# Stores on the ACT queue, loads on the SP queue, issued in pairs that GpSimd gates

## The chip, the cores and the metric

The kernel runs on one core of a Trainium2 chip. A core has compute engines that run independently of each other and meet through semaphores: VectorE (DVE in the profile), GpSimd (POOL), ScalarE (ACT) and TensorE (PE, not used here). SyncE (SP) does no arithmetic; it issues transfers. A transfer moves data between the chip's main memory (DRAM) and the core's on-chip memory, which has 128 partitions. An engine that issues a transfer puts it on its own queue, and the core's 16 DMA engines do the moving. A transfer has *landed* when all its parts have reported to a semaphore.

The metric is device time in microseconds, less being better.

## The reference

The input is a matrix of 8192 x 8192 numbers in float32. The reference is the gradient along a row:

```python
def reference(x):
    return np.gradient(x, axis=1)
```

For each row, an inner element of the result is `(x[j+1] - x[j-1]) / 2`. At the two borders it is the one-sided difference: `x[1] - x[0]` at the left and `x[m-1] - x[m-2]` at the right. 268.4 MB are read and as many written, and there is one subtraction and one halving for each element.

## The kernel before

Rows are cut into 32 sets of 256 rows. In a set each of the 128 partitions holds R = 2 neighbouring rows, so 16384 numbers or 64 KB. Three slots (NB = 3) hold the sets; set i lives in slot i % 3. A slot is 64 numbers longer than a set (SH = 64): the load puts its data at an offset of 64, and the result is written from offset 0 on in the same slot, so that each result is written behind the place still to be read.

A set goes through these steps, which all belong to slot i % 3:

1. The load (line 60, `load`), issued on SP's queue. It waits until the store of set i - 3, which used the same slot, has landed.
2. The border differences (line 70): GpSimd subtracts two numbers for each row, the left and the right border, into the small tile `ends`. This instruction is the one that waits for the load to land.
3. The inner differences (line 76): VectorE forms half the difference of the neighbours over the whole set in one instruction of 16382 elements for each partition. It waits for step 2.
4. The border copy (line 87): the two border numbers of each row are copied from `ends` into the result. VectorE does it in 20 sets, GpSimd in 12. It waits for step 3.
5. The store (line 89), issued on SP's queue. It waits for step 4.

The order is written out by hand (`tc.manual_schedule()`), and each engine takes its instructions in that order. The function `chain` tells the compiler's framework which earlier steps an instruction must wait for, so that no further waits are put in.

Loads and stores both stand on SP's one queue. The order on it is: loads 0, 1, 2; stores 0, 1, 2; loads 3, 4, 5; stores 3, 4, 5; and so on. The loads of the next three sets come after the third store of a group. An issue on SP whose wait isn't fulfilled holds up those behind it; transfers already issued go on.

Of the kernel before, what the change touches and what calls it, by code (L numbers as in the profile page):

```python
# [1 line left out]

# [4 lines left out]


@with_exitstack
def kernel(  # L10
    ctx: ExitStack,
    tc: tile.TileContext,
    x: bass.AP,
    out: bass.AP,
):

    nc = tc.nc
    P = nc.NUM_PARTITIONS
    n, m = x.shape
    R = 2
    NB = 3  # L30
    SH = 64
    W = R * m
    nsets = n // (P * R)
    f32 = x.dtype

    x_sets = x.rearrange("(s p t) m -> s p (t m)", p=P, t=R)
    out_sets = out.rearrange("(s p t) m -> s p (t m)", p=P, t=R)

    pool = ctx.enter_context(tc.tile_pool(name="pool", bufs=1))
    slots = [pool.tile([P, SH + W], f32, name=f"slot{k}", tag=f"slot{k}") for k in range(NB)]  # L40
    ends = pool.tile([P, nsets, R, 2], f32, name="ends", tag="ends")
    loads, stores = [], [None] * nsets
    in_front = {}

    def chain(i, ins, *needed):

        group, engine = f"slot{i % NB}", ins.ins.engine
        keep = [o.ins for o in needed]  # L50
        if in_front.get(engine, (None,))[0] == group:
            keep.append(in_front[engine][1])
        tc.declare_no_dep(ins.ins, group=group, keep=keep, reason="implied by the needed step")
        tc.add_to_no_dep_group(group, ins.ins)
        in_front[engine] = group, ins.ins
        return ins

    def load(i):
        b = slots[i % NB]
        ins = nc.sync.dma_start(out=b[:, SH : SH + W], in_=x_sets[i])  # L60
        loads.append(chain(i, ins, *([stores[i - NB]] if i >= NB else [])))

    with tc.manual_schedule():
        for i in range(NB):
            load(i)
        for i in range(nsets):
            b = slots[i % NB]
            xin = b[:, SH : SH + W].rearrange("p (t m) -> p t m", m=m)

            ins = nc.gpsimd.tensor_sub(  # L70
                out=ends[:, i, :, :],
                in0=xin[:, :, 1 : m : m - 2],
                in1=xin[:, :, 0 : m - 1 : m - 2],
            )
            at = [chain(i, ins, loads[i])]
            ins = nc.vector._custom_dve(  # L76
                dve_ops.TENSOR_TENSOR_REDUCE_SUB_MAX,
                out=b[:, 1 : W - 1],
                in0=b[:, SH + 2 : SH + W],
                in1=b[:, SH : SH + W - 2],  # L80
                s0=0.0,
                s1=0.5,
            )
            halved = chain(i, ins, *at)
            res = b[:, 0:W].rearrange("p (t m) -> p t m", m=m)
            placer = nc.gpsimd if i % 5 in (1, 3) and i < nsets - 2 else nc.vector
            ins = placer.tensor_copy(out=res[:, :, 0 : m : m - 1], in_=ends[:, i, :, :])  # L87
            placed = chain(i, ins, halved)
            ins = nc.sync.dma_start(out=out_sets[i], in_=b[:, 0:W])
            stores[i] = chain(i, ins, placed)  # L90
            if i % NB == NB - 1:
                for k in range(i + 1, min(i + 1 + NB, nsets)):
                    load(k)


# [1 line left out]
_INS = ['x']  # L97
_OUTS = [((8192, 8192), 'float32')]


# [23 lines left out]
```

## Time and profile before

| what | value |
|---|---|
| time, median of 3 runs | 1247.93 us (1247.32 to 1248.15) |
| span of the profiled execution, first to last instruction | 1245.7 us |
| moved | 268.44 MB read, 268.44 MB written |
| mean rate | 431 GB/s |
| VectorE busy | 554.6 us, 45% |
| GpSimd busy | 8.8 us, 1% |
| inner differences (line 76) | 32 x 17.224 us |
| issue to landing, median | load 58.0 us, store 40.4 us |

The profile is taken from one execution. The page gives that execution's span; no other time of it is given, and the median of the runs is 2.2 us above the span. "Idle" ahead of an instruction is time in which its engine had nothing to run, with the event that ended it. A queue's waits (SPq) are those of the sequencer that issues transfers. "Issue to landing" includes the time that a transfer stands behind others on its queue. In the timeline and the chain the first number is the start in microseconds from the beginning of the span, the second the duration. The DMA view counts packets: the pieces in which a DMA engine moves a transfer.

### The profile page before, as it was taken

What the parts mean: (1) busy time and instruction counts of PE and PEld (TensorE: products, weight loads), DVE (VectorE), ACT (ScalarE), POOL (GpSimd) and SP (SyncE); (2) the same over time, 40 slices, a digit from 0 to 9 for tenths busy, and PEclk for the clock granted to TensorE, in tenths of its full rate; (3) what the DMA queues carried; (4) which work ended last, traced back from release to release, by engine and by line L of the source; (5) the groups of instructions that cost most, each with busy time, mean ns of one, the idle gap of its engine ahead of it and who ended that gap; (6) DMA issues with size and microseconds to landing.
All of it is one profiled execution on the core that took longest, in us unless ns stands there. A gap on an engine that the chain in (4) does not pass through costs nothing.

```text
span 1245.7 us, 237 instructions
## 1 busy us (share of the span) xinstructions
DVE 554.6 (45%) x52; POOL 8.8 (1%) x48
## 2 busy tenths in 40 slices
DVE  2850583069009702850582079009603840591083
POOL 0000000000000000000000000000000000000000
DMA  9999999999999999999999999999999999999999
GB/s 404 438 436 423 427 431 438 438 438 436 436 427 431 425 438 436 425 434 436 429 434 436 434 436 434 436 434 438 419 436 436 434 438 438 431 434 429 429 410 404
DMA packets 9217, 536.88 MB, mean 431 GB/s; under 512 B 1024, under 2 KB 1024, under 8 KB 1024
## 3 DMA queue, kind: packets, MB, share of 16 engines
q1 hardware_dynamic: 9216, 536.88, 99.8%
q14 instruction: 1, 0.01, 0.0%
HBM read 268.44 MB, written 268.44 MB: 431 GB/s over the span
## 4 chain that ended last, share of the span: by engine, by line
another core or an unknown queue 74%; DVE 18%; DMA 3%; issue 2%; POOL 1%; SPq 0%; POOLq 0%
DVE slot L76 18%; DMA slot<-in_x_dram 3%; POOL ends L70 0%; POOL slot L87 0%; SPq L60 0%; POOLq L119 0%; DVE slot L87 0%
## 5 line engine op out<-in xcount | busy, mean ns | idle before, releaser
L76 DVE CUSTOM_DVE_ANT_0 slot<-slot 128x16382 f32<-128x16382 f32 x32 | 551.2, 17224 | 668.7 <-POOL ends L70 668.7
L70 POOL TENSOR_TENSOR ends<-slot 128x4 f32<-128x4 f32 x32 | 6.3, 198 | 989.6 <-DMA slot<-in_x_dram 989.6
L87 POOL COPY slot<-ends 128x4 f32<-128x4 f32 x12 | 2.3, 190 | 207.9 <-DVE slot L76 207.9
L87 DVE COPY slot<-ends 128x4 f32<-128x4 f32 x20 | 3.4, 172 | 0.7
L108 POOL MEMSET const-bfloat16-1.0<- 128x1 bf16 x1 | 0.1, 101 | 0.0
L108 POOL MEMSET const-uint8-127<- 128x1 uint8 x1 | 0.1, 101 | 0.0
L108 POOL MEMSET const-float32-0.0<- 128x1 f32 x1 | 0.1, 98 | 0.2 <-issue 0.2
L108 POOL MEMSET const-float32-1.0<- 128x1 f32 x1 | 0.1, 98 | 0.0
## 6 DMA issues: line engine op xcount, KB each, us to landing
slot<-in_x_dram SPq DMA_DIRECT2D x32, 58.0
out_dram<-slot SPq DMA_DIRECT2D x32, 40.4
```

Of the source, the lines that this page charges most:

```text
L70: ins = nc.gpsimd.tensor_sub(out=ends[:, i, :, :], in0=xin[:, :, 1 : m : m - 2], in1=xin[:, :, 0 : m - 1 : m - 2],)
L76: ins = nc.vector._custom_dve(dve_ops.TENSOR_TENSOR_REDUCE_SUB_MAX, out=b[:, 1 : W - 1], in0=b[:, SH + 2 : SH + W], in1=b[:, SH : SH + W - 2],
L87: ins = placer.tensor_copy(out=res[:, :, 0 : m : m - 1], in_=ends[:, i, :, :])
L108: nc = _bacc.Bacc("TRN2", target_bir_lowering=False, num_devices=1)
```

## The change

Three things change.

- Stores are issued on ScalarE's queue (`nc.scalar.dma_start`). Loads stay on SP's.
- Loads no longer go out in threes. Two are issued at the start; after that, the load of set i + 2 is issued beside the store of set i. The load itself has no wait on a store any more.
- GpSimd gates both. Before the border copy of set i (for i = 1 to 30) it does a small memset, `touch`, which waits until store i - 1 has landed. The border copy, which is now always GpSimd's, comes after it in GpSimd's order, and so does a second small memset for sets 0 to 29. The store waits for the border copy; the load waits for the second memset. The memsets write four numbers each in the free slot, in the region which the load then fills.

```diff
-    def load(i):
+    def load(i, *needed):
         b = slots[i % NB]
         ins = nc.sync.dma_start(out=b[:, SH : SH + W], in_=x_sets[i])
-        loads.append(chain(i, ins, *([stores[i - NB]] if i >= NB else [])))
+        loads.append(chain(i, ins, *needed))
+
+    def touch(i, at, *needed):
+        ins = nc.gpsimd.memset(slots[i % NB][:, at : at + 4], 0.0)
+        return chain(i, ins, *needed)
 
     with tc.manual_schedule():
-        for i in range(NB):
+        for i in range(NB - 1):
             load(i)
         for i in range(nsets):
...
             halved = chain(i, ins, *at)
             res = b[:, 0:W].rearrange("p (t m) -> p t m", m=m)
-            placer = nc.gpsimd if i % 5 in (1, 3) and i < nsets - 2 else nc.vector
-            ins = placer.tensor_copy(out=res[:, :, 0 : m : m - 1], in_=ends[:, i, :, :])
+            ahead = i + NB - 1
+            if 0 < i < nsets - 1:
+                touch(ahead, SH, stores[i - 1])
+            ins = nc.gpsimd.tensor_copy(out=res[:, :, 0 : m : m - 1], in_=ends[:, i, :, :])
             placed = chain(i, ins, halved)
-            ins = nc.sync.dma_start(out=out_sets[i], in_=b[:, 0:W])
+            ins = nc.scalar.dma_start(out=out_sets[i], in_=b[:, 0:W])
             stores[i] = chain(i, ins, placed)
-            if i % NB == NB - 1:
-                for k in range(i + 1, min(i + 1 + NB, nsets)):
-                    load(k)
+            if ahead < nsets:
+                load(ahead, touch(ahead, SH + 4))
```

## The prediction

> **What bounds the kernel now.** I read the page first, then the chain that ended last, then the waits, then single windows of the timeline and of the DMA view. The page settles the resource at once.
>
> ```profile
> span 1245.7 us, 237 instructions
> DVE 554.6 (45%) x52; POOL 8.8 (1%) x48
> DMA  9999999999999999999999999999999999999999
> DMA packets 9217, 536.88 MB, mean 431 GB/s; under 512 B 1024, under 2 KB 1024, under 8 KB 1024
> q1 hardware_dynamic: 9216, 536.88, 99.8%
> ```
>
> The reader should see that the 16 DMA engines never have a free slice, that everything runs on one queue (q1, SP's), and that VectorE is busy less than half the time. A transfer is 8.39 MB. There are 64 of them and 9216/64 = 144 packets in each: 9 for each engine, of which 8 are data (128 partitions of 64 KB over 16 engines) and one is the small packet at the end that reports the landing (64 x 16 = 1024 small ones). The timeline of the first set gives the pace.
>
> ```profile
> 0.74 1.33 SPq L60 DMA_DIRECT2D slot<-in_x_dram  x3
> 22.71 0.20 POOL L70 TENSOR_TENSOR ends<-slot 128x4 f32<-128x4 f32 x1 [22.27 <-DMA slot<-in_x_dram]
> 22.95 17.22 DVE L76 CUSTOM_DVE_ANT_0 slot<-slot 128x16382 f32<-128x16382 f32 x1 [22.95 <-POOL ends L70]
> 40.20 0.17 DVE L87 COPY slot<-ends 128x4 f32<-128x4 f32 x1
> 40.40 40.06 SPq L89 DMA_DIRECT2D out_dram<-slot  x3
> 42.04 0.20 POOL L70 TENSOR_TENSOR ends<-slot 128x4 f32<-128x4 f32 x1 [19.13 <-DMA slot<-in_x_dram]
> 59.56 0.19 POOL L87 COPY slot<-ends 128x4 f32<-128x4 f32 x1 [17.32 <-DVE slot L76]
> 62.44 0.20 POOL L70 TENSOR_TENSOR ends<-slot 128x4 f32<-128x4 f32 x1 [2.69 <-DMA slot<-in_x_dram]
> ```
>
> GpSimd's `ends` starts when a load has landed. Load 0 lands at 22.71, load 1 at 42.04, so a transfer that follows another on the queue takes 19.33 us, 2.416 us for a 64 KB packet of one engine. Load 2, behind which a store stands, takes 20.40. The chain shows the same place in a later set: 19.35 from the first load to the second, 20.05 to the third.
>
> ```profile
> 372.46 0.20 POOL ends L70
> 391.81 0.20 POOL ends L70
> 411.86 0.21 POOL ends L70
> ```
>
> Over the ten sets of three the third load's excess over the second is 1.07, 0.09, 0.18, 0.70, 0.52, 0.44, 0.11, 0.50, -0.01 and 0.01: 3.61 us in all. So the account of the span is: first landing 22.71, 63 more transfers at 19.33 (1217.8), together 1240.5; the last store lands at 1244.9, so 4.4 us are lost on the way, 3.6 of them at the change from loads to stores; then 0.8 of ending. The median of the three runs lies 1247.93 - 1245.7 = 2.2 us above the profiled span; the page gives no other time of that execution, and I add these 2.2 to every span below.
>
> The waits of SP's queue say why nothing is lost between transfers.
>
> ```profile
> SPq L89 <- DVE slot L87: 525.6, 20, 55.9
> SPq L60 <- DMA out_dram<-slot: 373.1, 29, 19.3
> SPq L89 <- POOL slot L87: 300.1, 12, 36.9
> ```
>
> SP waits almost always, but for one store or load while at least one other transfer lies on the queue, so its waits reach no DMA engine.
>
> **What the change can win.** Only the 4.4 us: no byte goes away. All of it would be 0.35%; a difference under 0.2% (2.5 us) can't be told from none by these runs.
>
> **What goes and comes at no cost.** The 20 border copies of VectorE (172 ns) become GpSimd's (190 ns): 18 ns each, behind transfers. The 60 memsets (touches) are new on GpSimd, at 0.10 us by the four constants' rows; 30 of them only follow the copy. Load 2 is no longer issued at 1.6 but at about 40.4, together with store 0. The ACT queue issues nothing now, so a store's issue there has no row; SP's rows are 332 to 424 ns, and it no longer stands in line with the loads. Behind the new waiting memset on GpSimd stand the border copy, the second touch and the next `ends`. The next load lands at about the time a pair is issued, `ends` and VectorE need 0.2 + 17.2 us, and the memset waits to the end of a pair of 2 x 19.33 = 38.7 us: VectorE is done some 20 us before the gate opens. If that cover went (a pair under 18 us), VectorE would be late next; it can't go, as a pair moves 16.8 MB.
>
> **What the gate adds.** Store k and load k+2 are issued when store k-1 has landed, 30 times (i = 1 to 30). In the old kernel something always lay behind the running transfer. Here only the rest of load k+1 does. Everything hangs on how much of it is left when store k-1 reports.
>
> How an engine serves two queues is shown by one event: the only packet of another queue in the span.
>
> ```profile
> DMA packets 16, 0.99 MB, mean 496 GB/s; under 512 B 0, under 2 KB 0, under 8 KB 0
> q1 hardware_dynamic: 15, 0.98, 114.2%
> q14 instruction: 1, 0.01, 1.0%
> ```
>
> This is the DMA view of the window 997 to 999. In the packet records the 8 KB instruction packet begins at 997.70, when one engine's 64 KB packet ends, and takes 0.31 us (1.0% of 32 engine-microseconds); the next 64 KB packet of that engine, in the middle of store 24, follows it and takes 2.69 instead of 2.42. So an engine turns to another queue after each 64 KB packet, and moves one packet at a time. A pair then goes store, load, store, load. If both begin on an idle engine, eight of each alternate, and the store's small reporting packet must wait for its turn behind the load's eighth packet. Both land together and the queues are empty. Do they begin so? Load 1 leaves its engines at about 41.0 to 41.6 (landing at 42.04, less the 0.4 us between the end of the last packet and the wait that sees it, as at the last store in the packet records). Store 0 is issued at 40.40, and the first load needed 1.0 us from its issue to its first packet: 41.4. So most engines are idle or about to be, and the alternation starts with no lead.
>
> The price of a gap, from rows: the first load was issued on an idle queue at 0.74 and landed at 22.71, 21.97 us, of which 19.33 are full pace: 2.64 for issue, first packet and landing. The smallest such value is the last store's, 20.9 less 19.33 = 1.6, part of it behind store 30. Between landing and issue lie GpSimd's memset 0.10, the border copy 0.19, and the hand-over 0.03, with a hand-over ahead of them of the same kind: 0.35. A gap is 1.95 to 3.0; I take 2.5, the middle, because the store comes first and its pace has no idle-queue row of its own. 30 x 2.5 = 75 (58 to 90). The 3.6 at the change to stores go, as in-queue changes end. 1245.7 + 75 - 3.6 = 1317, with 2.2: 1319. At the end nothing new: store 30 runs while VectorE does set 31, as now (load 31's `ends` at 1206.28, store 31's issue at 1224.0).
>
> **The price with no row: changing from load to store inside a pair.** Each engine does it 8 times in 31 pairs, 248 times. Ends: -0.01 to 1.07 us each by the ten sets, so 0 to 265; the packet after the instruction packet cost 0.27, which would be 67. A gain below nothing I exclude: packets of both kinds keep 2.42 us alike, so an engine's pace is the same either way. I take 0 for the point: in the last two sets, when engines had drifted apart, the change cost 0.0. The 0.27 row is nearer in kind, but it is one event, so it is a rival at full weight rather than part of the sum.
>
> **A page against the row.** The Trainium skill, "DMA: Bandwidth & Descriptors", section "Queues, rings and completion order", says an engine goes round its queues but drains a whole packet, typically 9 to 17 descriptors, before it switches. If that meant the nine descriptors of a transfer here, store and load would follow one another whole, the store would land 19 us ahead, no gap would open, and the sum would be 1244 to 1255; the one event in store 24 speaks against it, and I go by the event. The same page, "Issuing engines are not separate DMA queues", says that issuing from several engines saves only issue time: by it nothing is to be won.
>
> **The rivals.**
> - Gap and change both cost: 1319 + 67 = 1386. For it: the 2.69 us packet. Against: it is one packet, and the change was free in the last sets.
> - Not slower: the store's report goes with its eighth data packet, with no turn of its own. Then the store lands one packet, 2.42 us, ahead of the load. The way from its last packet to the next first packet is 0.4 + 0.35 + 1.0 = 1.75 us, less than 2.42, so no engine runs dry, as long as engines stand less than 0.67 apart. 1247.9 - 3.6 = 1244.3. It decides at that 0.67: load 1's ends were 0.6 apart.
> - The same with the change costing 0.27: 1244.3 + 67 = 1311.
> - The change doesn't do what it says: an engine finishes a queue's whole share before it turns, so the pair is no pair but store, load, as on one queue. 1244.3, and with 31 changes at the mean 0.36 it is 1255.
>
> **How the numbers follow.** Gap alone 40 in 100 (own range 1302 to 1334); gap and change 20; lead holds and change costs 8; lead holds free 13 (8 faster, 4 same, 1 slower); whole shares 12 (3 faster, 4 same, 5 slower); anything else, such as changes at 0.1 or over 0.4 us, 7, slower. Faster 11, same 8, slower 81. Range 1244 to 1390: below it lie about 5 (the free lead with the rest of the 4.4 us), above it about 12 (the dear half of the second case).
>
> **What would show it.** In the changed profile: gaps between pairs as a mean rate of about 408 GB/s (536.88 MB in 1317 us) instead of 431, first `ends` of consecutive sets about 41.2 us apart, a store's issue to landing of about 40 us and a load's about the same. If stores land about 2.4 us before loads and the period is 38.7, the lead holds. If stores land after about 21 us, shares drain whole. If the period is above 43, the change from load to store costs. I am wrong if the report needs no turn of its own, or if a mix of reads and writes moves faster than 19.33 us for 8.39 MB.

## The result, and the profile after

The changed kernel takes 1636.5 us (1634.0 to 1642.7 in five runs), against 1247.9 before. The ratio is 1.312, with a 95% interval of 1.310 to 1.314. The direction was forecast; the size was not: 1319 was predicted, with a range of 1244 to 1390. The profiled execution has a span of 1640.9 us, 395 more than before.

The page of the changed kernel, its size, its DMA queues and the issues:

```profile
span 1640.9 us, 323 instructions
DMA packets 9217, 536.88 MB, mean 327 GB/s; under 512 B 1024, under 2 KB 1024, under 8 KB 1024
q1 hardware_dynamic: 4608, 268.44, 47.2%
q10 hardware_dynamic: 4608, 268.44, 40.4%
slot<-in_x_dram SPq DMA_DIRECT2D x32, 51.5
out_dram<-slot ACTq DMA_DIRECT2D x32, 51.7
```

The bytes and packets are those of before, in equal parts on SP's queue (q1, loads) and ACT's (q10, stores). The shares give two losses. They add up to 87.6% of the 16 engines' span where it was 99.8%, so an engine is idle for 12% of the span on the mean, some 200 us. And the packets are slower. A share times 16 engines times the span, over 4096 data packets, is the mean time of a 64 KB packet: 0.472 x 16 x 1640.9 / 4096 = 3.03 us for a load's, 0.404 in its place 2.59 us for a store's, where it was 2.42. A load and the store beside it take the same time to land, 51.5 and 51.7 us.

One pair in the timeline:

```profile
92.65 0.10 POOL L53 MEMSET slot<- 128x4 f32 x1 [50.54 <-DMA out_dram<-slot]
92.69 0.19 POOL L82 COPY slot<-ends 128x4 f32<-128x4 f32 x1
92.81 0.10 POOL L53 MEMSET slot<- 128x4 f32 x1
92.91 52.59 ACTq L84 DMA_DIRECT2D out_dram<-slot  x2
92.94 52.55 SPq L49 DMA_DIRECT2D slot<-in_x_dram  x2
144.88 0.10 POOL L53 MEMSET slot<- 128x4 f32 x1 [51.80 <-DMA out_dram<-slot]
```

GpSimd's gate waits 50.5 us and then 51.8, and the store and the load are issued 0.03 us apart. From gate to gate it is 52.2 us, where two transfers at full pace need 38.7. The packet records (start, duration, queue and size of every packet) of pairs 0 to 29 split a pair, on the mean over pairs:

| step of a pair | us |
|---|---|
| 16 packets at full pace | 38.7 |
| packets slower than that (8 x 3.06 + 8 x 2.60) | 6.6 |
| start of the first packets, and what lies between packets | 1.3 |
| wait of the mean engine for the slowest (46.6 to 50.2) | 3.6 |
| from the last landing report to the next pair's first packet | 1.8 |
| sum | 52.0 |

The excess is 13.3 us a pair, about 400 us for 30; less the 3.6 us of old changes from load to store, that is the measured 395. The records don't name the engine of a packet, but they can be chained, as one packet begins where another ends. So read, the packets of an engine alternate, load, store, load, store, and its two landing reports come within about 0.01 us of each other. In the 29 pairs from pair 1 to 29 the first packet on all 16 engines is the load's, though the store was issued 0.03 us earlier; the store's eighth packet is the last, with the load's report and then the store's right behind it.

VectorE's work stays hidden, as the waits of the changed kernel say. GpSimd's border difference waited for a load only at the two loads of the start:

```profile
POOL slot L53 <- DMA out_dram<-slot: 1545.5, 30, 52.6
POOL ends L63 <- DMA slot<-in_x_dram: 23.7, 2, 22.2
```

### The profile page after: what moved, and what is told of

The parts are those of the page before. It is cut to its first block, busy times and chain, and to the rows that moved or that the text cites. A ratio compares the mean times of both kernels' runs of the same rounds, so it can differ in the third digit from the quotient of the medians.

```text
span 1640.9 us, 323 instructions
## 1 busy us (share of the span) xinstructions
DVE 551.1 (34%) x32; POOL 13.5 (1%) x128
## 4 chain that ended last, share of the span: by engine, by line
another core or an unknown queue 94%; DMA 2%; issue 1%; POOL 1%; SPq 0%; POOLq 0%
DMA slot<-in_x_dram 2%; POOL ends L63 0%; POOL slot L53 0%; POOL slot L82 0%; SPq L49 0%; POOLq L113 0%
## 5 line engine op out<-in xcount | busy, mean ns | idle before, releaser
L53 POOL MEMSET slot<- 128x4 f32 x60 | 6.1, 101 | 1545.5 <-DMA out_dram<-slot 1545.5
L82 POOL COPY slot<-ends 128x4 f32<-128x4 f32 x32 | 6.1, 190 | 34.6 <-DVE slot L69 34.6
## 6 DMA issues: line engine op xcount, KB each, us to landing
slot<-in_x_dram SPq DMA_DIRECT2D x32, 51.5
out_dram<-slot ACTq DMA_DIRECT2D x32, 51.7
```

The costliest lines, as they stand in the source:

```text
L53: ins = nc.gpsimd.memset(slots[i % NB][:, at : at + 4], 0.0)
L82: ins = nc.gpsimd.tensor_copy(out=res[:, :, 0 : m : m - 1], in_=ends[:, i, :, :])
```

## Experiments

### First theory: alternating on two queues is slow, and the gate adds a gap

Four kernels, each with one part of the change taken back or alone. The first puts the stores on SP's queue and keeps the gate.

```diff
-            ins = nc.scalar.dma_start(out=out_sets[i], in_=b[:, 0:W])
+            ins = nc.sync.dma_start(out=out_sets[i], in_=b[:, 0:W])
```

> The changed kernel with the gate, the memsets and the pairs as they are, but the stores back on SP's queue, each store ahead of the load beside it. On one queue the two can't alternate. Theory A (most of the loss of 389 us comes from the two queues being served in turn, and the gate costs because both transfers then end together): the store lands after about 20 us of a pair, the next pair is issued while the load still moves, nothing runs dry, and the time falls to 1244 to 1256 us (the lower end is 1247.9 less the 3.6 us of the old changes from load to store, the upper adds 31 changes at 0.36 us). Rival B (the gate through GpSimd costs by itself, whatever the queues): above 1300 us.

Measured: 1250.3 us (1248.9 to 1251.9), ratio 1.0021 (1.0012 to 1.0030). The gate, the memsets and the pairs cost 2.4 us by themselves; rival B falls. The store lands after 38.4 us, not 20, since the load of the pair before still lies ahead of it, but the queue never runs empty.

The second is the same on one queue with the load ahead of the store, so that the last transfer on the queue opens the gate.

```diff
-            ins = nc.scalar.dma_start(out=out_sets[i], in_=b[:, 0:W])
-            stores[i] = chain(i, ins, placed)
             if ahead < nsets:
                 load(ahead, touch(ahead, SH + 4))
+            ins = nc.sync.dma_start(out=out_sets[i], in_=b[:, 0:W])
+            stores[i] = chain(i, ins, placed)
```

> As the changed kernel, but both transfers on SP's queue with the load ahead of the store, so that the store that opens the gate is the last on the queue: a gap at each of 30 pairs and no alternation. Theory A: only the round trip from landing to first packet is left, 1.95 to 3.0 us at each of 30 gates by the prediction's rows, so 1247.9 + 58 to 90 = 1306 to 1338 us. Rival B (the dry gap itself is what costs 13 us a pair): about 1636 us.

Measured: 1369.0 us, ratio 1.097 (1.096 to 1.099): 121 us, 4.0 at each of 30 gates, above the forecast 1.95 to 3.0. The packet records give the rest: besides some 2.2 us in which an engine is idle, the first load packet of a pair takes 0.7 us more than 2.42 and the load's last packet, ahead of the store, 1.2 more. So this is what running empty costs on one queue, and it is far from 13.

The third leaves two queues and takes the gate away.

```diff
-            if 0 < i < nsets - 1:
-                touch(ahead, SH, stores[i - 1])
...
-                load(ahead, touch(ahead, SH + 4))
+                load(ahead, *([stores[i - 1]] if i else []))
```

> Two queues as in the changed kernel, no gate: a store goes out when its border copy is done, a load when the store that frees its slot has landed. The packets of both queues still alternate on each engine, but an engine that is done early has further work behind. Theory A: the alternation alone stays, by the packet durations of the changed kernel's records (about 2.60 us for a store's packet and 3.06 for a load's, against 2.42): 31 pairs of 8 x 5.66 = 45.3 us, about 1245 + 31 x 6.6 = 1450 us, and the wait for the slowest engine goes. Rival B (the gate is the cause): back near 1250 us. Rival C (the alternation is all of it, and the gate costs nothing more): near 1636 us.

Measured: 1253.1 us, ratio 1.0050 (1.0028 to 1.0072). Theory A falls here, and rival C with it. The page's queue lines of this run:

```profile
span 1256.1 us, 263 instructions
q1 hardware_dynamic: 4608, 268.44, 49.5%
q10 hardware_dynamic: 4608, 268.44, 49.3%
```

0.495 x 16 x 1256.1 / 4096 is 2.43 us a packet, and the records show load, store, load, store on each engine, at 2.418 us in the median of either kind. Alternating packet by packet costs next to nothing: the whole kernel is 5 us above the one before.

The fourth has no computation and no waits between the kinds: loads into two slots in turn, stores of a third slot of zeros. These lines stand in place of the old loop.

```diff
...
+        nc.gpsimd.memset(slots[2][:, 0:W], 0.0)
+        for i in range(nsets):
+            nc.sync.dma_start(out=slots[i % 2][:, 0:W], in_=x_sets[i])
+            nc.scalar.dma_start(out=out_sets[i], in_=slots[2][:, 0:W])
...
```

> No computation: 32 loads on SP's queue into two slots in turn and 32 stores of a third slot, which holds zeros, on ACT's queue, all as large as before. The result isn't the gradient. No transfer waits on one of the other kind, and each queue always holds another transfer. Theory A: the two queues alternate packet by packet and it takes about 1245 + 31 x 6.6 = 1450 us, loads' packets about 3.06 us and stores' 2.60. Rival B (gates and waits on landings are the cause, and two busy queues move at full pace): 1240 to 1250 us.

Measured: 1261.0 us, the median of ten runs: three at 1245, one at 1255.5 and six from 1260 to 1265. The packets are again near 2.42. In the profiled run, one of the long ones, 14 engines end within 1.6 us of each other and the other two some 19 and 20 us later. The spread of a store's 16 reports grows from 1.4 to 22 us over that run, and the end waits for the last engine. The median is above rival B's 1240 to 1250, but theory A's 1450 is far off: two queues alternate freely.

### Second theory: it takes both queues running empty

If alternating is free and the gate is free, it must be the two together: both queues end at once at each gate and are filled again together. First, VectorE was taken out.

```diff
-            ins = nc.vector._custom_dve(
...
-            halved = chain(i, ins, *at)
-            res = b[:, 0:W].rearrange("p (t m) -> p t m", m=m)
+            halved = at[0]
+            res = b[:, SH : SH + W].rearrange("p (t m) -> p t m", m=m)
...
-            ins = nc.scalar.dma_start(out=out_sets[i], in_=b[:, 0:W])
+            ins = nc.scalar.dma_start(out=out_sets[i], in_=b[:, SH : SH + W])
```

> The changed kernel without VectorE's work: gate, two queues and pairs stay, the border copy writes into the loaded data and the store sends that. The result isn't the gradient. Theory D (the loss comes of the two queues both running empty at each gate and being filled again together; VectorE has no part in it): about 1636 us, between 1600 and 1660. Rival V (VectorE's reads and writes of on-chip memory slow the packets): clearly shorter, near 1400 us or below, and packets near 2.42 us.

Measured: 1588.9 us, in two runs. VectorE has no part in the slow pace (rival V falls). The time is below the 1600 to 1660 of theory D, and the run shows why, and how the kernel gets there. Without VectorE's 17 us the first store starts early, with the loads still far from done. Windows of about one pair each; the last two columns are the DMA share and GB/s:

```profile
30.00:70.00 40.00, 0.46 (x4) 1.00 1.02 441
70.00:114.00 44.00, 0.47 (x4) 1.00 0.99 429
114.00:158.00 44.00, 0.46 (x4) 1.00 0.99 429
158.00:206.00 48.00, 0.56 (x5) 1.00 0.86 350
206.00:258.00 52.00, 0.07 (x1) 1.00 0.87 323
258.00:311.00 53.00, 0.84 (x8) 1.00 0.86 317
```

For three pairs all is at full pace, and then it falls to the changed kernel's. By the packet records an engine's load reports 27, 19, 9, 2 and then 0 us after the store of its pair: between one store's report and the next store's first packet the engine serves loads alone, and the load catches up at each gate. Once it has caught up, both queues are empty at the gate, and it stays so. The changed kernel starts without that lead.

Next, free streams, without gates or computation, that start together on empty queues (a dry start) and never run empty again. These lines too stand in place of the old loop.

```diff
...
+        nc.sync.dma_start(out=slots[2][:, 0:W], in_=x_sets[0])
+        nc.gpsimd.tensor_copy(out=slots[0][:, 0:4], in_=slots[2][:, 0:4])
+        for i in range(nsets):
+            nc.scalar.dma_start(out=out_sets[i], in_=slots[2][:, 0:W])
+            if i + 2 < nsets:
+                nc.sync.dma_start(out=slots[i % 2][:, 0:W], in_=x_sets[i + 2])
...
```

> No gates and no computation: one load, and when it has landed a stream of 30 loads on SP's queue and a stream of 32 stores on ACT's start together on empty queues, as a pair of the changed kernel does, and go on without ever running empty. The result isn't the gradient. Theory D: the packets are slow (about 3.1 and 2.6 us) only after the common start, for some tens of us, and then settle at 2.42: the total is 1245 to 1275 us. Rival Y (a load and a store that start together and go in step stay slow for good, as they always touch the same piece of their sets): 30 pairs of 45 to 50 us, 1400 to 1500 us.

Measured: 1227.7 us for 63 transfers, one less than the expected 1245 to 1275 allowed for. On each engine the first two packets take 3.1 to 4.2 us, the others 2.42. Rival Y falls. This run was read as a sign for theory D; a later run shows how narrow it was.

Then the gate itself, with sets of half the size (R = 1, six slots), so that a pair can be issued while the one before still moves.

```diff
-    R = 2
-    NB = 3
+    R = 1
+    NB = 6
...
-        for i in range(NB - 1):
+        for i in range(NB - 2):
...
-            ahead = i + NB - 1
-            if 0 < i < nsets - 1:
-                touch(ahead, SH, stores[i - 1])
+            ahead = i + NB - 2
+            if 2 <= i < nsets - 1:
+                touch(ahead, SH, stores[i - 2])
```

> Sets of half the size (32 KB packets, 64 sets, six slots); two queues, pairs and GpSimd's gate as in the changed kernel, but the gate of pair i waits for store i-2, not i-1, so a whole pair is still moving when the next is issued. The small sets alone cost GpSimd and VectorE nothing that shows. Theory D (running empty is the cause): 1245 to 1265 us. Rival Q (issuing store and load together on two queues is the cause, empty or not): over 1400 us.

> As the run with the gate two back, but the gate waits for store i-1 as in the changed kernel: both queues run empty at each of 62 gates. Theory D: each gate costs again what it cost with large sets, 389/30 = 13 us, if the cost belongs to the empty start (62 x 13 = 800, about 2050 us), or half of it in the slow packets, if these are slow by the byte: 62 x (13 - 6.6/2) = 600, about 1850 us. Rival Q: the same time as the run with the gate two back.

The second of the two has the same sizes and the gate on store i - 1, with NB - 1 in both places of the diff. Measured: 1247.3 us with the gate two back (ratio 0.9997, 0.9987 to 1.0007) and 1445.8 us with the gate one back. Queue lines of the page, first two back, then one back:

```profile
q1 hardware_dynamic: 9216, 268.44, 50.0%
q10 hardware_dynamic: 9216, 268.44, 49.9%
```

```profile
q1 hardware_dynamic: 9216, 268.44, 47.5%
q10 hardware_dynamic: 9216, 268.44, 43.1%
```

So the emptying is needed for the loss: one gate's depth is worth 198 us, and rival Q falls. But the price was wrong. It is 3.2 us on the mean of 62 gates, neither 13 nor 10; the first six still had loads left, and over the 56 that found every engine idle it is 3.5. With 32 KB packets only a load's first packet after such a gate is slow (2.4 us instead of 1.21), the others keep pace, and the engines end a pair within 0.7 us of each other. Something more makes the large pieces slow for a whole pair.

### What keeps the 64 KB packets slow

The streams that settled had their first store issued 0.25 us ahead of the load; the changed kernel has 0.03. Three kernels varied the start and the size of the pieces, which is the size of a data packet. The first: the free streams with the load ahead, by a GpSimd memset that the stores also wait for.

```diff
+        nc.gpsimd.memset(slots[2][:, 0:600], 0.0)
         for i in range(nsets):
-            nc.scalar.dma_start(out=out_sets[i], in_=slots[2][:, 0:W])
             if i + 2 < nsets:
                 nc.sync.dma_start(out=slots[i % 2][:, 0:W], in_=x_sets[i + 2])
+            nc.scalar.dma_start(out=out_sets[i], in_=slots[2][:, 0:W])
```

> As the run of free streams after a common dry start, but the load starts first: ACT's stores also wait for a small GpSimd memset of about 0.5 us. The result isn't the gradient. What is asked is why the packets in a pair of the changed kernel stay slow for all 46 us, when those of the free streams settled after two packets. Theory O (the order: in the changed kernel the load's packet moves first, in the free streams the store's did): the packets stay slow well beyond the first two, and the total is above 1260 us, up to 1450. Rival K (one transfer on each queue is too little stock for pieces of 64 KB, whatever the order): settles after two packets again, 1225 to 1235 us, as 63 transfers are moved.

Measured: 1231.3 us, two slow packets on each engine and then 2.42. That the load is first doesn't by itself make the packets slow. But the start differs from the changed kernel's in another way: with the load 0.67 us ahead, each engine moves two load packets before the first store packet.

The second: the changed kernel, the memset that releases the load 2400 numbers wide (`touch` gets the width as a parameter).

```diff
...
-                load(ahead, touch(ahead, SH + 4))
+                load(ahead, touch(ahead, SH + 4, n=2400))
```

> The changed kernel with the second memset, which lets the load go, made 600 times as wide (about 2 us), so that at each gate the store's packets start first. Theory O: packets settle to 2.42 us after the first, a pair takes 38.7 us and a gate 4 to 6 us more: 1370 to 1430 us. Rival K: the packets stay slow, 1620 to 1690 us.

Measured: 1298.9 us, ratio 1.041 (1.038 to 1.044). Holding the load back by 2 us at each gate makes the kernel 338 us shorter. Rival K falls, one transfer on each queue is enough. The time is below theory O's range, too: with a later load the store also gets a lead, and the store's report comes on the mean 3.4 us ahead of the load's. So the 16 engines hardly run empty together: the 1.7 us a gate are nearly all slow packets at the start of a pair. The page and the timeline of this run; the memset of 128 x 2400 is the delay:

```profile
q10 hardware_dynamic: 4608, 268.44, 49.7%
q1 hardware_dynamic: 4608, 268.44, 49.5%
```

```profile
402.06 0.10 POOL L53 MEMSET slot<- 128x4 f32 x1 [37.06 <-DMA out_dram<-slot]
402.23 2.10 POOL L53 MEMSET slot<- 128x2400 f32 x1
402.33 41.58 ACTq L84 DMA_DIRECT2D out_dram<-slot  x2
404.36 41.57 SPq L49 DMA_DIRECT2D slot<-in_x_dram  x2
443.31 0.10 POOL L53 MEMSET slot<- 128x4 f32 x1 [38.61 <-DMA out_dram<-slot]
```

The third: the same pairs of 16.8 MB with each transfer issued as two halves of 32 KB pieces. The stores are cut in the same way, and the gate waits for both halves.

```diff
-        ins = nc.sync.dma_start(out=b[:, SH : SH + W], in_=x_sets[i])
-        loads.append(chain(i, ins, *needed))
+        halves = []
+        for t in range(R):
+            ins = nc.sync.dma_start(
+                out=b[:, SH + t * m : SH + t * m + m], in_=x_sets[i][:, t * m : t * m + m]
+            )
+            halves.append(chain(i, ins, *needed))
+        loads.append(halves)
...
```

> The changed kernel with each transfer issued as two halves of 32 KB pieces on the same queue, pairs of the same 16.8 MB as before; the gate waits for both halves of the store. Rival S (the size of the piece: with 32 KB, as with the small sets, only the first packet after a gate is slow): 1248 + 30 x 3.2 to 5 us = 1345 to 1400 us. Theory O: the load's packet still goes first, so near 1636 us. Rival K: two transfers stand on each queue now, so the slow packets go for most of a pair, 1350 to 1450 us.

Measured: 1355.0 us, 3.6 us a gate, with only the first load packet of a pair slow (2.4 us). Rival S holds; this run alone doesn't tell it from rival K, which the run before had refuted.

### The start, isolated

Free streams once more, now with the changed kernel's own start: GpSimd's copy releases the store, and a small memset right behind it the load. The edit is against the first free streams. No queue ever runs empty after that.

```diff
-        nc.gpsimd.tensor_copy(out=slots[0][:, 0:4], in_=slots[2][:, 0:4])
+        nc.gpsimd.tensor_copy(out=slots[2][:, 0:4], in_=slots[2][:, 4:8])
+        nc.gpsimd.memset(slots[0][:, 0:4], 0.0)
```

> Free streams after a common dry start once more, with the start given as in the changed kernel: GpSimd's small copy lets the store go and its small memset, right behind, the load. Each queue always holds further transfers. The result isn't the gradient. Theory O2 (the alternation load, store, load, store from a dry start with 64 KB pieces is what stays slow, and keeps itself slow): the packets stay at about 3.1 and 2.6 us for 46 us and longer, total 1240 to 1450 us. Rival K2 (slow packets need one transfer on each queue, with nothing behind): two or three slow packets, 1225 to 1235 us for 63 transfers.

Measured: 1530.9 us, against 1227.7 for the same 63 transfers with the earlier start. The timeline of the two starts, first this one, then the one that settled:

```profile
22.65 0.19 POOL L34 COPY slot<-slot 128x4 f32<-128x4 f32 x1 [22.21 <-DMA slot<-in_x_dram]
22.77 0.10 POOL L35 MEMSET slot<- 128x4 f32 x1
22.86 2.33 ACTq L37 DMA_DIRECT2D out_dram<-slot  x4
22.90 0.80 SPq L39 DMA_DIRECT2D slot<-in_x_dram  x2
```

```profile
22.55 2.86 ACTq L36 DMA_DIRECT2D out_dram<-slot  x4
22.58 0.19 POOL L34 COPY slot<-slot 128x4 f32<-128x4 f32 x1 [22.14 <-DMA slot<-in_x_dram]
22.80 0.80 SPq L38 DMA_DIRECT2D slot<-in_x_dram  x2
```

The store and the load are issued 0.04 us apart in the one and 0.25 in the other. The DMA lines of the pages, in the same order:

```profile
DMA packets 9072, 528.49 MB, mean 346 GB/s; under 512 B 1008, under 2 KB 1008, under 8 KB 1008
q1 hardware_dynamic: 4464, 260.05, 48.1%
q10 hardware_dynamic: 4608, 268.44, 45.6%
```

```profile
DMA packets 9072, 528.49 MB, mean 431 GB/s; under 512 B 1008, under 2 KB 1008, under 8 KB 1008
q10 hardware_dynamic: 4608, 268.44, 50.6%
q1 hardware_dynamic: 4464, 260.05, 49.1%
```

Over 1529.1 us and 3968 and 4096 data packets the slow one has 2.97 us for a load's and 2.72 for a store's packet, and it stays so from the start to the end of the loads. So two streams of 64 KB pieces have two paces, and 0.2 us at the start chose between them. With it went the order of the first packets: in the slow run each engine began with a load's packet and alternated from there, in the settled one with a store's. Rival K2 falls. Theory O2 named the slow pace rightly, but its 1240 to 1450 us were too low: the pace lasted to the end.

Is it the order or the coincidence? In the changed kernel itself, a delay of half a microsecond was tried in both orders: the load later (the same edit as for 2 us, with n=600), and the store later, behind a memset on a scratch tile.

> The changed kernel with the second memset 150 times as wide (about 0.5 us instead of 2 us). If the lead of the store's first packet is what matters, half a microsecond is enough, since the first packet is decided by who comes first: near the 1299 us of the run with 2 us. If the load must come later than the whole slow first packet of the store (3 us), half a microsecond changes little: above 1500 us.

```diff
+    scratch = pool.tile([P, 600], f32, name="scratch", tag="scratch")
...
+            if ahead < nsets:
+                load(ahead, touch(ahead, SH + 4))
+                nc.gpsimd.memset(scratch[:, :], 0.0)
             ins = nc.gpsimd.tensor_copy(out=res[:, :, 0 : m : m - 1], in_=ends[:, i, :, :])
...
-            if ahead < nsets:
-                load(ahead, touch(ahead, SH + 4))
```

> The changed kernel with the load let go first at each gate and the store about 0.6 us later, behind a wide GpSimd memset on a scratch tile. If what matters is that both queues start within some tens of ns of each other (the engines then fall out of step), this order is as good as the other: 1300 to 1360 us. If the store must be first, it stays near 1636 us.

Measured: 1331.3 us with the load 0.53 us later and 1365.1 us with the store 0.66 us later, against 1636.5 with 0.03 between them. One pair's issues and the queue lines, the load later first:

```profile
414.71 0.34 ACTq L84 DMA_DIRECT2D out_dram<-slot  x1
415.24 0.33 SPq L49 DMA_DIRECT2D slot<-in_x_dram  x1
q1 hardware_dynamic: 4608, 268.44, 49.4%
q10 hardware_dynamic: 4608, 268.44, 48.2%
```

```profile
425.46 0.33 SPq L50 DMA_DIRECT2D slot<-in_x_dram  x1
426.12 0.34 ACTq L88 DMA_DIRECT2D out_dram<-slot  x1
q1 hardware_dynamic: 4608, 268.44, 49.1%
q10 hardware_dynamic: 4608, 268.44, 45.4%
```

The first is 32 us above the forecast 1299, the second 5 us above its range, but both are far from the slow pace: after two or three slow packets at the start of a pair an engine is at 2.42 us. So neither queue has to be first. In both kernels each engine begins with two packets of the queue that is ahead. Whether it is the coincidence that makes the pace slow, or the strict load, store, load, store from the first packet that came with it in both slow kernels, these runs don't part. What is left, 83 and 117 us, is 2.8 and 3.9 us at each gate: the price of running empty, slow first packets included (1.9 and 1.7 us). With the load later the store reports 2.2 us ahead of it, which covers part of the gap; with the store later nothing does.

Last, the free streams with the changed kernel's start and 32 KB pieces (R = 1).

> The free streams with the start given as in the changed kernel, with sets of half the size, so pieces of 32 KB (64 sets; one load less than stores is moved by half a set). The result isn't the gradient. If the slow state belongs to any two streams that start together, it stays slow: about 1530 us. If it needs pieces of 64 KB, as the runs with halves suggest: 1230 to 1240 us.

Measured: 1239.3 us, packets at pace, though here too each engine began with a load's packet and alternated from there. In these runs the slow pace came only where both were given: a start within 0.04 us on empty queues and pieces of 64 KB. Starts between 0.04 and 0.25 us apart were not tried.

## Why the prediction failed

**Right.** The bound was read rightly: DMA engines without a gap, on one queue. The work of VectorE and GpSimd stayed hidden. An engine does turn to the other queue after each 64 KB packet, as the one instruction packet in store 24 had shown, and no pair drained whole. The Trainium skill, "DMA: Bandwidth & Descriptors", section "Queues, rings and completion order", speaks of a packet of typically 9 to 17 descriptors drained before a switch; these runs, with one 64 KB packet of each queue in turn, differ, and the measurement decides. The gap is real: both transfers land together, and both queues are empty at every gate. But they do so the other way round than was predicted. The load's packet goes first, the store's eighth is the last, and it is the load's report that waits behind it. So the store was last whether or not a report takes a turn of its own, and that the gap came as forecast is in part luck. That a report does take its own turn is shown by the run with the load half a microsecond later: there the store's report comes after its eighth packet and one load packet more. "No lead at the start" held, and the rivals in which a lead or a whole share covers the gap didn't occur in the changed kernel.

**The gap's size.** 1.95 to 3.0 us were worked out. The runs that kept pace but ran empty show 2.8 (with part of the gap covered), 3.6, 3.9 and 4.0; the one with the load 2 us later, 1.7, hardly ran empty. In the changed kernel itself the rows of the pair give 1.8 and 1.3, 3.1 us. The term was somewhat small: its 2.64 holds one slow first packet, as a single queue showed it, but with two queues two or three 64 KB packets of an engine are slow after a gate, and on one queue a load's last packet ahead of a store is slow again (1.2 us). With 3.6 to 4.0, the prices of the halves and of the one queue, the sum would have been 1356 to 1368, against the 1331 and 1365 that the changed kernel takes once its two issues are held half a microsecond apart.

**The step that failed** is the sentence that "packets of both kinds keep 2.42 us alike, so an engine's pace is the same either way". It was drawn from a trace in which one queue was served, and used for two queues that start together. Pace was a term of the sum only as a price for the change from load to store; that price is indeed zero (no gate, or free streams: 2.42). What came instead is a pace of 3.06 and 2.60 for the whole pair, 6.6 us more than the 38.7 of full pace, and, because the engines then end 6 us apart, 3.6 us in which the mean engine waits for the slowest before the gate can open. The second had no term at all: the sum treated 16 engines as one. A gate that waits for a transfer waits for its slowest engine.

**The instruction packet's 0.27 us** was made into a rival of 67 us. One event isn't a price: 248 such changes in the kernel without the gate cost next to nothing (1253.1 us against 1247.9).

**The range** ended at 1390, though the sum's own bound for the price with no row, 265 us, reached 1584. The end was set by one row, the 0.27, instead of by the bound; the slow packets, 30 x 6.6 = 198 us, lie within it, but even the bound would not have held 1636, for want of the wait for the slowest engine (30 x 3.6 = 108 us).

## What to carry to other kernels

On a kernel whose DMA engines are always busy, ask of every new wait what still lies on the queues when it opens: with a transfer left behind it the wait was nearly free here (2.4 us for all 30 gates on one queue), without one it cost 3 to 4 us each time, and 13 in the changed kernel. When a wait is on a whole transfer, count the slowest of the 16 engines, not the mean. And don't start two large transfers on two queues at the same instant from empty: half a microsecond between them, in either order, or pieces of half the size, was worth 271 to 305 us here.

## What the runs showed that was not expected

Two streams on two queues with 64 KB packets can stand at two paces, 431 and 346 GB/s with the same transfers, and keep the one that they start with: free streams issued 0.04 us apart stayed at 346 for 1.5 ms, issued 0.25 or 0.67 us apart, two runs each, they stayed at about 430. With 32 KB packets the start 0.03 us apart gave 431.

What is inside the slow pace stays open. The records show one thing that goes with it. In the slow free streams, from 100 to 1150 us, between 3 and 13 of the 16 engines are loading at any time, while most of the others store. In those that settled, the number swings between 0 and 16 from packet to packet: now all load, now all store. A mixture alone isn't the cause, though: in the run with the start 0.25 us apart 6 to 10 engines are loading for about half of the time, at 2.42 us a packet. Which resource the engines meet at, and whether the size of a piece or its position in memory decides, was not tried.
